# A four-layer decoder trunk on one core: the residual held with features on partitions

## The chip, the core and the metric

The kernel runs on one core of a Trainium2 chip. The core has five engines that run side by side and meet at semaphores: TensorE (PE, matrix products, with its weight loads shown apart as PEld), VectorE (DVE), ScalarE (ACT), GpSimd (POOL) and SyncE (SP), which here only issues DMAs. Each engine works through its own queue in order. TensorE writes to PSUM, which has eight banks of 512 float32 columns on 128 partitions. The metric is device time in microseconds (us) of one execution.

## The reference, cut to what matters

Input and output are 256 tokens of 1024 features, in float32. Layer 0 and layer 3 mix tokens by retention, layer 1 by block attention (with 256 tokens it is plain causal attention), layer 2 by differential attention.

```python
for i in range(DEPTH):                       # 4 layers
    h = _rmsnorm(x, norm1[i])                # over the 1024 features of a token
    m = mixer_i(h)                           # retention, attention, differential attention, retention
    x = x + m                                # m = (...) @ w_out
    x = x + _squared_relu_mlp(_rmsnorm(x, norm2[i]), w_up[i], w_down[i])

def _squared_relu_mlp(h, w_up, w_down):      # 1024 -> 4096 -> 1024
    u = jax.nn.relu(h @ w_up)
    return (u * u) @ w_down
```

## The kernel before

**Precision.** Every weight matrix is read in float32 and split on the chip into a high part (`whi`, ACT, line 170) and a rest (`wlo`, DVE, line 180). Each product takes three passes (`passes`, lines 323 to 326): high by high, high by rest, rest by high. The other operand is split in the same way: `xhi`, `xlo` for the normed input, `uh`, `ul` for the hidden layer, `oh`, `ol` for a mixer's output.

**Weights.** They come in pieces of 128 x 1024 words in a fixed order (`specs`). `advance` lets the split run up to four pieces ahead of the piece that TensorE takes (`take`).

**Products.** Up projection and retention's q and k (`mm_a`) hold a block of weights in the array (128 x 128) and stream the 256 tokens past it: 256 columns for each matmul. The projections to v, gate, q, k, v (`mm_b`) and the down and output projections (`mm_o`) hold a block of activations and stream 512 columns of weights. So `mm_o` leaves its sums (`acc`, four banks) with tokens on partitions, in quarters of 128 tokens x 512 features.

**Residual.** `X` holds 128 partitions x (2 halves of the tokens) x 1024 features. `finish` (lines 436 to 457) runs the last three pieces of a down or output projection quarter by quarter, adds each quarter to `X` on DVE (line 448, or 450 with the factor `r2` of the MLP's norm), and puts off a `norm_quarter` by two ticks. That transposes the quarter on TensorE (line 299, four transposes of 128 x 128 in a stop), and makes `xhi` (ACT, line 302) and `xlo` (DVE, line 305) from the transposed bank. The norm's factor is put in later: for a mixer through `me`, `r2`, `r` (one value for each token, on the token's partition), for an MLP as `r2` in `finish`. `rms` takes the sums of squares on ACT (line 311), each token's along its partition, three ticks after `finish`.

**Order.** The code emits each engine's queue in one pass. `tick()` advances a counter, about once for each piece; `later(n, fn)` puts a step n ticks off, and `at` puts one at a tick counted from the start of an attention layer. Steps due in one tick run in the order of the table `ORDER`. In attention, `softmax` for a pair of heads emits four matmuls (`sc`), four DVE operations that add the bias and take the row's extreme (line 731), and four exponentials on ACT (line 734); the eight pairs start at ticks 12 to 15 and 19, 19, 20, 21. The values `vt` are copied out of PSUM by ACT (line 841) after the projection's last piece, and `av_moba` or `av_diff` on TensorE need them.

Of the kernel before, what the change touches and what calls it, by code (L numbers as in the profile page):

```python
# [31 lines left out]
def trunk(ctx, tc, x_in, rel_bias, norm1, norm2, w_up, w_down, ret_w_in, ret_w_out,  # L32
          moba_w_in, moba_q_norm, moba_k_norm, moba_w_out,
          diff_w_in, diff_q_norm, diff_k_norm, diff_lambda, diff_subln, diff_w_out,
# [5 lines left out]
    const = ctx.enter_context(tc.tile_pool(name="const", bufs=1))  # L40
    op_ = ctx.enter_context(tc.tile_pool(name="op", bufs=1))
    xp = ctx.enter_context(tc.tile_pool(name="xp", bufs=1))
    up_ = ctx.enter_context(tc.tile_pool(name="up", bufs=1))
    wp = ctx.enter_context(tc.tile_pool(name="wp", bufs=1))
# [7 lines left out]
    NRAW, NPC = 3, 6  # L52

# [10 lines left out]
    ORDER = {"av_moba": 0, "av_diff": 0, "probs_t": 1, "softmax": 2, "qk_t": 4, "qk_norm": 5}  # L64
# [21 lines left out]
    def hi_lo(i, a, b, narrow):  # L86
        n = a * b
        hi = wp.tile([P, n], F32R, tag="hi", name="whi", bufs=NPC)
        odd = i % 2
        lo = wp.tile([P, n + (32 if odd else 96)], F32R, tag="lo%d" % (i % NPC), name="wlo", bufs=1)  # L90
        o = 0 if odd == narrow else (32 if odd else 96)
        return (t.rearrange("p (a b) -> p a b", a=a) for t in (hi, lo[:, o:o + n]))

# [66 lines left out]
    def split_piece():  # L160
# [7 lines left out]
        hi, lo = hi_lo(i, a // 2, b, a == 8)  # L168
# [33 lines left out]
    rows = mp.tile([32, P], F32, tag="t2k", name="rows", bufs=4)  # L202
    X = const.tile([P, 2, D], F32, name="X")
    xf = x_in.rearrange("b s d -> (b s) d")
    warm = const.tile([P, 1], F32, name="warm")
    junk = const.tile([P, D], mybir.dt.bfloat16, name="junk")
# [6 lines left out]
    xv = xf.rearrange("(t p) d -> p t d", p=P)  # L213
    ACT.dma_start(rows, norm1.rearrange("l (c p) -> (l c) p", p=P))
    nc.sync.dma_start(X[:, :, 0:S], xv[:, :, 0:S])
    ACT.dma_start(ident, c_ident)
    load_raw(0, 4)
    ACT.activation(warm, warm, AF.Copy)
    for i in range(1, 4):
        nc.sync.dma_start(X[:, :, i * S:(i + 1) * S], xv[:, :, i * S:(i + 1) * S])  # L220
        load_raw(i, 4)
# [5 lines left out]
    nc.sync.dma_start(kd0[:, 2:6, :], rd[:, 2:6, :])  # L227

# [6 lines left out]
    rows2 = mp.tile([64, P], F32, tag="t2k", name="rows2", bufs=4)  # L235

    def small_loads():
        POOL.dma_start(rb, rel_bias)
        POOL.memset(rows2, 0.0)
        POOL.dma_start(rows2[0:32, :], norm2.rearrange("l (c p) -> (l c) p", p=P))  # L240
        for i, w in enumerate((moba_q_norm, moba_k_norm, diff_q_norm, diff_k_norm)):
            for g in range(2):
                POOL.dma_start(rows2[32 + i:33 + i, g * HD:(g + 1) * HD], w)
        POOL.dma_start(rows2[36:37, :], diff_subln)

    W = const.tile([P, 96], F32, name="W")
    wps = aux_bank("wps")
    PE.transpose(wps[:, :32], rows, ident[:32, :32])
    DVE.tensor_copy(W[:, :32], wps[:, :32])
# [3 lines left out]
    def head_weights():  # L253
        wps2 = aux_bank("wps2")
        PE.transpose(wps2[:, :64], rows2, ident[:64, :64])
        DVE.tensor_copy(W[:, 32:96], wps2[:, :64])
# [9 lines left out]
    def small(name, shape):  # L266
        return mp.tile(shape, F32, tag="sm_" + name, name=name, bufs=3)
# [25 lines left out]
    def norm_quarter(l, which, c, t):  # L293
        tt = slice(t * P, (t + 1) * P)
        for pair in range(2):
            ps = aux_bank("xt")
            for i in range(2):
                k = c * 4 + pair * 2 + i
                PE.transpose(ps[:, i * P:(i + 1) * P], X[:, t, k * P:(k + 1) * P], ident)
            for i in range(2):  # L300
                k = c * 4 + pair * 2 + i
                ACT.activation(st["hi"][:, k, tt], ps[:, i * P:(i + 1) * P], AF.Copy, scale=wn(l, which, k))
            for i in range(2):
                k = c * 4 + pair * 2 + i
                DVE.scalar_tensor_tensor(st["lo"][:, k, tt], ps[:, i * P:(i + 1) * P], wn(l, which, k),
                                         st["hi"][:, k, tt].bitcast(F32), op0=OP.mult, op1=OP.subtract)

    def rms(which):
        ss = small("ss", [P, 2])
        for t in range(2):  # L310
            ACT.activation(junk, X[:, t, :], AF.Square, accum_out=ss[:, t:t + 1])
        me = small("me", [P, 2])
        POOL.tensor_scalar(me, ss, 1.0 / D, EPS, op0=OP.mult, op1=OP.add)
# [4 lines left out]
        if which == 0:  # L318
            r = small("r", [P, 2])
            rsqrt(r, me, "r", POOL)  # L320
            st["r"] = r
# [20 lines left out]
    def first_qk(ps):  # L342
# [4 lines left out]
        def turn(pr):  # L347

            bank = aux_bank("xt")
            for i in range(2):  # L350
                for t in range(2):
                    c0 = i * S + t * P
                    k = 2 * pr + i
                    PE.transpose(bank[:, c0:c0 + P], X[:, t, k * P:(k + 1) * P], ident)
            for i in range(2):
                k = 2 * pr + i
# [546 lines left out]
```

## Time and profile before

| | |
|---|---|
| median of 3 runs | 1349.3 us (1347.78 to 1349.87) |
| the profiled execution, time | 1350.42 us |
| its span, first to last instruction | 1348.6 us |
| TensorE busy | 1335.3 us (99%) |
| VectorE busy | 840.4 us (62%) |
| ScalarE busy | 688.2 us (51%) |
| mean granted clock | 0.997 |

The profiled execution took 1.1 us more than the median, and 1.8 us of it lie outside its span. In the trace a matmul's duration is longer than the distance to the next one, because matmuls follow each other in the array before the earlier is through; what a stream of them costs is read from the distance of their starts. A row of a timeline gives start, duration, engine, line, operation, `out<-in` tiles, shapes and count, and in brackets how long the engine had been idle before and what ended that.

### The profile page before, as it was taken

The page shows a single profiled execution, that of the slowest core. Times are in us where ns is not written, and L with a number is a line of the kernel's source. Part 1 is how long each engine was busy: PE and PEld are TensorE (multiplying, and loading weights), DVE is VectorE, ACT ScalarE, POOL GpSimd, SP SyncE. Part 2 cuts the span into 40 slices and gives each one's busy share as a digit, 9 for nine tenths or more (in the row PEclk, how much of TensorE's full clock was granted, in tenths as well). Part 3 has the DMA queues.
Part 4 walks back from the last instruction along what each step waited for, and adds up shares of the span by engine and source line. Part 5 has one row for each costly group of instructions (what it writes and reads, how often), then busy time and mean ns, then how long its engine had stood idle before and what let it go on. Part 6 is the DMA issues. An engine that isn't in the chain of part 4 may idle for free.

```text
span 1348.6 us, 19835 instructions
## 1 busy us (share of the span) xinstructions
PE 1335.3 (99%) x8029; PEld 1170.5 (87%) x8029; DVE 840.4 (62%) x1235; ACT 688.2 (51%) x1058; POOL 109.6 (8%) x314
## 2 busy tenths in 40 slices
PE   9999999999999999999999999999999999999998
PEld 7888889999987679999987789999988888899997
DVE  6666647555568756555578676555667675565554
ACT  5454436444456646444466754444455444554442
POOL 3111100000031000000021110000031011000000
PEclk9999999999999999999999999999999999999999
DMA  8544565555554346555554346555564555465551
GB/s 299 186 163 159 182 193 168 196 198 199 202 202 150 125 125 223 187 188 188 187 173 140 125 147 226 189 188 188 179 205 144 183 172 188 149 225 199 191 189 63
DMA packets 141389, 242.28 MB, mean 180 GB/s; under 512 B 4336, under 2 KB 89024, under 8 KB 141296
## 3 DMA queue, kind: packets, MB, share of 16 engines
q1 hardware_dynamic: 139248, 237.78, 52.7%
q0 software_dynamic: 1072, 2.35, 0.6%
q8 instruction: 63, 1.03, 0.3%
q10 hardware_dynamic: 976, 0.87, 0.2%
q14 instruction: 30, 0.25, 0.1%
HBM read 239.91 MB, written 1.07 MB: 179 GB/s over the span
## 4 chain that ended last, share of the span: by engine, by line
PE 93%; DVE 3%; ACT 2%; DMA 1%; issue 1%; DVEq 0%; ACTq 0%
PE acc L324 12%; PE acc L325 12%; PE acc L326 12%; PE up L325 9%; PE up L326 9%; PE up L324 9%; PE vg L324 4%; PE vg L326 4%; PE vg L325 4%; PE qkv L324 2%; PE qkv L326 2%; PE qkv L325 2%; PE qk L324 2%; PE qk L325 2%; PE qk L326 2%; ACT e L734 1%
## 5 line engine op out<-in xcount | busy, mean ns | idle before, releaser
L180 DVE TENSOR_TENSOR wlo<-raw,whi 128x1024 fp32r<-128x1024 f32 (+1 forms) x448 | 527.3, 1217 | 107.3 <-ACT whi L170 99.5
L170 ACT ACTIVATE whi<-raw 128x1024 fp32r<-128x1024 f32 (+1 forms) x448 | 449.9, 1048 | 88.8 <-PE acc L326 66.7
L324 PE MATMUL up<-xhi,whi 128*128 128x256 f32 x1024 | 283.9, 277 | 0.0
L325 PE MATMUL up<-xlo,whi 128*128 128x256 f32 x1024 | 283.7, 277 | 0.0
L326 PE MATMUL up<-xhi,wlo 128*128 128x256 f32 x1024 | 283.4, 277 | 0.0
L324 PE MATMUL acc<-whi,uu 128*128 128x512 f32 x512 | 200.0, 391 | 0.0
L325 PE MATMUL acc<-wlo,uu 128*128 128x512 f32 x512 | 199.6, 390 | 0.0
L326 PE MATMUL acc<-whi,uu 128*128 128x512 f32 x512 | 199.6, 390 | 0.0
L325 PEld LDWEIGHTS up<-xlo,whi 128*128 128x128 f32 x1024 | 192.3, 188 | 2.2
L324 PEld LDWEIGHTS up<-xhi,whi 128*128 128x128 f32 x1024 | 192.3, 188 | 2.2
L326 PEld LDWEIGHTS up<-xhi,wlo 128*128 128x128 f32 x1024 | 192.5, 188 | 0.0
L466 DVE SCALAR_TENSOR_TENSOR u<-up,u 128x512 f32<-128x512 f32 x64 | 44.2, 691 | 203.3 <-ACT u L465 203.1
L465 ACT ACTIVATE u<-up 128x512 f32<-128x512 f32 x64 | 38.0, 595 | 240.6 <-PE up L326 240.6
L326 PEld LDWEIGHTS acc<-whi,uu 128*128 128x128 f32 x512 | 96.1, 188 | 20.3
L324 PEld LDWEIGHTS acc<-whi,uu 128*128 128x128 f32 x512 | 96.2, 188 | 17.7
L325 PEld LDWEIGHTS acc<-wlo,uu 128*128 128x128 f32 x512 | 96.1, 188 | 17.7
L324 PE MATMUL vg<-whi,xhi 128*128 128x512 f32 x256 | 100.6, 393 | 0.0
L325 PE MATMUL vg<-wlo,xhi 128*128 128x512 f32 x256 | 99.9, 390 | 0.2 <-DVE wlo L180 0.2
L326 PE MATMUL vg<-whi,xlo 128*128 128x512 f32 x256 | 99.8, 390 | 0.0
L324 PE MATMUL qkv<-whi,xhi 128*128 128x512 f32 x192 | 79.0, 411 | 0.0
L324 PE MATMUL acc<-whi,oh 128*128 128x512 f32 x192 | 76.5, 398 | 0.0
L326 PE MATMUL qkv<-whi,xlo 128*128 128x512 f32 x192 | 75.6, 394 | 0.0
(228 smaller groups left out, 1808.0 us busy)
## 6 DMA issues: line engine op xcount, KB each, us to landing
raw<-in_w_up_dram SPq DMA_DIRECT2D x64, 1024.0 KB, 5.6
raw<-in_w_down_dram SPq DMA_DIRECT2D x64, 1024.0 KB, 6.1
raw<-in_ret_w_in_dram SPq DMA_DIRECT2D x45, 1024.0 KB, 5.2
raw<-in_ret_w_out_dram SPq DMA_DIRECT2D x16, 1024.0 KB, 4.9
raw<-in_moba_w_in_dram SPq DMA_DIRECT2D x12, 1024.0 KB, 5.2
raw<-in_diff_w_in_dram SPq DMA_DIRECT2D x12, 1024.0 KB, 5.2
raw<-in_moba_w_out_dram SPq DMA_DIRECT2D x4, 1024.0 KB, 4.9
raw<-in_diff_w_out_dram SPq DMA_DIRECT2D x4, 1024.0 KB, 4.8
```

Source lines behind the costliest of these rows:

```text
L170: ACT.activation(hi[:, part], half[:, part], AF.Copy)
L180: DVE.tensor_tensor(lo[:, part], half[:, part], hi[:, part].bitcast(F32), op=OP.subtract)
L324: PE.matmul(ps, lhsT=ah, rhs=bh, start=first, stop=False, skip_group_check=True)
L325: PE.matmul(ps, lhsT=ah, rhs=bl, start=False, stop=False, skip_group_check=True)
L326: PE.matmul(ps, lhsT=al, rhs=bh, start=False, stop=last, skip_group_check=True)
L465: ACT.activation(u, ps, AF.Relu)
L466: DVE.scalar_tensor_tensor(u, ps, 0.0, u, op0=OP.max, op1=OP.mult)
L734: ACT.activation(e[:, hh, :], e[:, hh, :], AF.Exp, bias=nm[:, qt, hh:hh + 1], scale=-1.0, accum_out=sm[:, qt, hh:hh + 1])
```

## The change

- `x` is handed over transposed (`x_t`), and the output is transposed back on the host. `X` is 128 partitions x 8 blocks of features x 256 tokens, all through. The norms' weights come as one array (`cols`) that is already laid out by partition; the small loads and transposes for them are gone.
- `mm_o` now holds a 128 x 128 block of weights and streams 256 tokens, as `mm_a` does: 24 matmuls of 256 columns for a piece instead of 12 of 512. `acc` has features on partitions, and `finish` goes by quarters of two blocks of features.
- The transposes of the norm are gone. `norm_part` makes `xhi` and `xlo` straight from `X`, in `finish` itself, right behind the quarter's addition; `squares` squares the quarter on ACT.
- The sum over features now runs across partitions. `rms` adds the four squared quarters on DVE, and `rms_sum`, one tick later, has TensorE sum over partitions with a matrix of ones: for an MLP one matmul of 256 columns, whose result on all partitions becomes `r2b`; for a mixer two matmuls of one column.
- An MLP's factor `r2b` varies along the free axis, so `finish` takes two DVE operations for a quarter (multiply, add) where one was.
- In attention the bias step (`logits`) and the exponentials (`softmax`) are apart. The first four pairs of heads keep their ticks; of the last four the exponentials move from ticks 19, 19, 20, 21 to 20, 20, 21, 21.
- Pools are laid out anew, some with gaps, and small tiles changed place.

TensorE where retention ends and the MLP begins (`acc` are its banks, `oh`, `ol` retention's output); before, inside `finish`:

```order
L325 MATMUL acc<-wlo,oh 128x512
L326 MATMUL acc<-whi,ol 128x512
L299 MATMUL xt<-ident,X 128x128 x4
L324 MATMUL acc<-whi,oh 128x512
L325 MATMUL acc<-wlo,oh 128x512
```

And after the change, in the middle of the first block of the up projection, 24 matmuls behind `finish`:

```order
L333 MATMUL up<-xhi,whi 128x256
L334 MATMUL up<-xlo,whi 128x256
L335 MATMUL up<-xhi,wlo 128x256
L315 MATMUL ms<-sq,ones 128x256
L333 MATMUL up<-xhi,whi 128x256
```

The four stops for transposes are gone from the stream, and one matmul on the sums of squares stands in it, ahead of the other half of the up projection's first block.

DVE where layer 1's MLP ends and layer 2 begins (`lam`, `ld`, `nl` belong to the differential factor); before, from the last quarter's addition on:

```order
L450 SCALAR_TENSOR_TENSOR X<-acc,r_4851,X 128x512
L305 SCALAR_TENSOR_TENSOR xlo<-xt,W,xhi 128x128 x4
L642 SCALAR_TENSOR_TENSOR junk,ld<-lam 128x64 x2
L646 TENSOR_TENSOR nl<-ld 128x1
L647 TENSOR_SCALAR nl<-nl 128x1
L305 SCALAR_TENSOR_TENSOR xlo<-xt,W,xhi 128x128 x4
L180 TENSOR_TENSOR wlo<-raw,whi 128x1024 x4
```

After the change:

```order
L446 TENSOR_TENSOR sc<-acc,r2b 128x512
L447 TENSOR_TENSOR X<-X,sc 128x512
L296 SCALAR_TENSOR_TENSOR xlo<-X,W,xhi 128x256 x2
L643 SCALAR_TENSOR_TENSOR junk,ld<-lam 128x64 x2
L647 TENSOR_TENSOR nl<-ld 128x1
L648 TENSOR_SCALAR nl<-nl 128x1
L308 TENSOR_TENSOR sq<-sq 128x512 x3
L309 TENSOR_TENSOR sq<-sq 128x256
L323 TENSOR_SCALAR me<-ms 128x2
```

The four additions of squares stand behind everything else of the last quarter, and `ms`, on TensorE, needs the last of them.

ACT around the first copy of the values in layer 1 (`kT` are the last keys, `e` exponentials, `oh` the first pair's output); before:

```order
L707 ACTIVATE kT<-qkT,W 128x4x128 x2
L734 ACTIVATE e,sm<-e,nm 128x128 x2
L734 ACTIVATE e,sm<-e,nm 128x256 x2
L734 ACTIVATE e,sm<-e,nm 128x128 x2
L734 ACTIVATE e,sm<-e,nm 128x256 x2
L170 ACTIVATE whi<-raw 128x1024
L841 ACTIVATE vt<-qkv,r 128x512 x2
L783 ACTIVATE oh<-oT 128x256
```

After:

```order
L708 ACTIVATE kT<-qkT,W 128x4x128 x2
L176 ACTIVATE whi<-raw 128x1024
L847 ACTIVATE vt<-qkv,r 128x512 x2
L789 ACTIVATE oh<-oT 128x256
L741 ACTIVATE e,sm<-e,nm 128x128 x2
L741 ACTIVATE e,sm<-e,nm 128x256 x2
```

Eight exponentials have moved from ahead of the copy to behind it.

The core of the diff:

```diff
-    def norm_quarter(l, which, c, t):
-        ... (transposes on PE, xhi on ACT, xlo on DVE from the bank)
+    def norm_part(l, which, q):
+        for k in (2 * q, 2 * q + 1):
+            ACT.activation(st["hi"][:, k, :], X[:, k, :], AF.Copy, scale=wn(l, which, k))
+        for k in (2 * q, 2 * q + 1):
+            DVE.scalar_tensor_tensor(st["lo"][:, k, :], X[:, k, :], wn(l, which, k),
+                                     st["hi"][:, k, :].bitcast(F32), op0=OP.mult, op1=OP.subtract)
+
+    def squares(q):
+        sq = mp.tile([P, 512], F32, tag="pe", name="sq", bufs=9)
+        ACT.activation(sq, X[:, 2 * q:2 * q + 2, :].rearrange("p k s -> p (k s)"), AF.Square)
+        st["sq", q] = sq
 
     def rms(which):
-        ss = small("ss", [P, 2])
+        ss = st["sq", 0]
+        for q in range(1, 4):
+            DVE.tensor_tensor(ss, ss, st["sq", q], op=OP.add)
+        DVE.tensor_tensor(ss[:, :S], ss[:, :S], ss[:, S:], op=OP.add)
+        later(1, rms_sum, which, ss)
+
+    def rms_sum(which, ss):
+        ps = aux_bank("ms")
+        if which == 1:
+            PE.matmul(ps[:, :S], lhsT=ones, rhs=ss[:, :S], start=True, stop=True)
+            DVE.tensor_scalar(r2b, ps[:, :S], 1.0 / D, EPS, op0=OP.mult, op1=OP.add)
+            DVE.reciprocal(r2b, r2b)
+            return
         for t in range(2):
-            ACT.activation(junk, X[:, t, :], AF.Square, accum_out=ss[:, t:t + 1])
+            PE.matmul(ps[:, t:t + 1], lhsT=ss[:, t * P:(t + 1) * P], rhs=ones[:, 0:1], start=True, stop=True,
+                      skip_group_check=True)
...
-    def mm_o(q, piece, src, first, last):
-        c, t = q
+    def mm_o(c, piece, src, first, last):
+
         hi, lo = piece
         uh, ul = src
-        tt = slice(t * P, (t + 1) * P)
-        cc = slice(c * 512, (c + 1) * 512)
-        passes(st["acc"][q], uh[:, tt], ul[:, tt], hi[:, 0, cc], lo[:, 0, cc], first, last)
+        cc = slice(c * P, (c + 1) * P)
+        half = slice(c % 2 * S, (c % 2 + 1) * S)
+        passes(st["acc"][c // 2][:, half], hi[:, 0, cc], lo[:, 0, cc], uh, ul, first and c % 2 == 0, last and c % 2 == 1)
...
-        for q in QUARTERS:
+        for q in range(4):
             for i, (pc, src) in enumerate(zip(pcs, srcs)):
-                mm_o(q, pc, src, False, i == len(srcs) - 1)
...
+                for c in (2 * q, 2 * q + 1):
+                    mm_o(c, pc, src, False, i == len(srcs) - 1)
+            xs = X[:, 2 * q:2 * q + 2, :]
+            ps = st["acc"][q].rearrange("p (k s) -> p k s", k=2)
+            if mlp_out:
+                sc = mp.tile([P, 2, S], F32, tag="t2k", name="sc", bufs=4)
+                DVE.tensor_tensor(sc, ps, r2b.unsqueeze(1).to_broadcast([P, 2, S]), op=OP.mult)
+                DVE.tensor_tensor(xs, xs, sc, op=OP.add)
+            else:
                 DVE.tensor_tensor(xs, ps, xs, op=OP.add)
...
-                later(2, norm_quarter, nxt_norm[0], nxt_norm[1], c, t)
+                norm_part(nxt_norm[0], nxt_norm[1], q)
+                squares(q)
             tick()
         if nxt_norm is not None:
-            later(3, rms, nxt_norm[1])
+            later(1, rms, nxt_norm[1])
...
-        SM0, AV0 = ((12, 13, 14, 15), (19, 19, 20, 21)), (20, 24)
+        LG, EX, AV0 = ((12, 13, 14, 15), (19, 19, 20, 21)), ((12, 13, 14, 15), (20, 20, 21, 21)), (20, 24)
```

## Rows read from the trace of the kernel before

**Rows 1.** The page: busy time by engine, and the chain's shares.

```profile
PE 1335.3 (99%) x8029; PEld 1170.5 (87%) x8029; DVE 840.4 (62%) x1235; ACT 688.2 (51%) x1058; POOL 109.6 (8%) x314
...
PE 93%; DVE 3%; ACT 2%; DMA 1%; issue 1%; DVEq 0%; ACTq 0%
```

**Rows 2.** Timeline, TensorE in an MLP: first matmuls of three neighbouring groups.

```profile
260.50 0.39 PE L324 MATMUL acc<-whi,uu 128*128 128x512 f32 x1
...
265.96 0.28 PE L324 MATMUL up<-xhi,whi 128*128 128x256 f32 x1
...
271.43 0.39 PE L324 MATMUL acc<-whi,uu 128*128 128x512 f32 x1
```

**Rows 3.** Timeline, TensorE in retention: second matmul of 48, and what follows.

```profile
53.75 0.28 PE L325 MATMUL qk<-xlo,whi 128*128 128x256 f32 x1
...
59.35 0.39 PE L324 MATMUL vg<-whi,xhi 128*128 128x512 f32 x1
```

**Rows 4.** Timeline, TensorE from retention to the MLP of layer 0.

```profile
199.85 0.60 PE L299 MATMUL xt<-ident,X 128*128 128x128 f32 x4
200.21 0.47 PE L324 MATMUL acc<-whi,oh 128*128 128x512 f32 x1
200.52 0.39 PE L325 MATMUL acc<-wlo,oh 128*128 128x512 f32 x1
...
206.37 0.68 PE L299 MATMUL xt<-ident,X 128*128 128x128 f32 x4
206.80 0.37 PE L324 MATMUL up<-xhi,whi 128*128 128x256 f32 x1
```

**Rows 5.** Waits of TensorE (us in total, times, longest).

```profile
PE oT L778 <- ACT vt L841: 2.6, 1, 2.6
PE od L797 <- ACT vt L841: 2.5, 1, 2.5
```

**Rows 6.** Timeline, ACT ahead of the first copy of values in layer 1.

```profile
449.20 0.40 ACT L734 ACTIVATE e<-e,nm 128x128 f32<-128x128 f32 x1 [2.19 <-DVE nm L731]
...
453.67 1.24 ACT L841 ACTIVATE vt<-qkv,r 128x512 f32<-128x512 f32 x2
```

**Rows 7.** Windows behind both waits: PE, PEld, DVE, ACT, POOL busy, granted clock (PEclk), DMA, GB/s.

```profile
456.10:459.50 3.40, 3.40 (x10) 2.60 (x9) 3.30 (x19) 2.81 (x9) 0.00 (x0) 0.50 0.85 304
...
749.70:753.00 3.30, 3.30 (x17) 3.30 (x17) 0.44 (x1) 0.92 (x5) 0.00 (x0) 0.50 0.55 139
```

**Rows 8.** Timeline, DVE: the second addition behind TensorE's quarter, layer 0.

```profile
200.05 0.69 DVE L448 TENSOR_TENSOR X<-acc,X 128x512 f32<-128x512 f32 x1 [1.35 <-PE acc L326]
```

**Rows 9.** Groups by line and shape, DVE (count, busy us, mean ns of one).

```profile
L471 DVE TENSOR_TENSOR uu<-u,uu 128x512 fp32r<-128x512 f32 x64 | 44.4, 693 | 44.7 <-ACT uu L470 44.7
...
L448 DVE TENSOR_TENSOR X<-acc,X 128x512 f32<-128x512 f32 x16 | 11.1, 692 | 17.6 <-PE acc L326 17.6
...
L746 DVE SCALAR_TENSOR_TENSOR e<-e,dc 128x256 f32<-128x256 f32 x8 | 3.8, 480 | 0.0
...
L784 DVE TENSOR_TENSOR ol<-oT,oh 128x256 fp32r<-128x256 f32 x8 | 3.4, 424 | 10.0 <-ACT oh L783 10.0
```

**Rows 10.** The same view, ACT.

```profile
L357 ACT ACTIVATE xhi<-xt,W 128x256 fp32r<-128x256 f32 x8 | 3.4, 472 | 4.6 <-PE xt L354 4.6
```

**Rows 11.** Timeline, TensorE: full float32 products, four records of 256 columns, four of 128.

```profile
26.84 1.55 PE L523 MATMUL s<-qk 128*128 128x256 f32 x8 [0.20 <-DVE qk L514]
28.14 0.48 PE L324 MATMUL vg<-whi,xhi 128*128 128x512 f32 x1
```

**Rows 12.** Timeline, DVE: the differential factor at the start of layer 2.

```profile
681.58 0.22 DVE L642 SCALAR_TENSOR_TENSOR junk<-lam 128x64 bf16<-128x64 f32 x1
...
682.54 0.15 DVE L647 TENSOR_SCALAR nl<-nl 128x1 f32<-128x1 f32 x1
```

**Rows 13.** Timeline: the first product of the program (TensorE), the last addition (DVE).

```profile
7.75 0.39 PE L376 MATMUL qk<-xhi,whi 128*128 128x256 f32 x1 [0.96 <-ACT whi L365]
...
1344.46 0.75 DVE L450 SCALAR_TENSOR_TENSOR X<-acc,r,X 128x512 f32<-128x512 f32 x1 [1.29 <-PE acc L326]
```

More of the change, by code (lines that the diff above doesn't have):

```diff
@@ L212, in trunk @@
     DVE.memset(warm, 0.0)
[L213 to L216, printed above, removed]
+    DVE.memset(ones, 1.0)
+    ACT.dma_start(W, cols)
+    nc.sync.dma_start(X[:, 0:2, :], xv[:, 0:2, :])
     load_raw(0, 4)
@@ L317, in rms @@
         st["r2"] = r2
[L318 to L321, printed above, removed]
+        r = small("r", [P, 2])
+        rsqrt(r, me, "r", POOL)
+        st["r"] = r
     def passes(ps, ah, al, bh, bl, first, last):
@@ L347, in turn @@
         def turn(pr):
[L349 to L356, printed above, removed]
-                ACT.activation(st["hi"][:, k, :], bank[:, i * S:(i + 1) * S], AF.Copy, scale=wn(0, 0, k))
-            for i in range(2):
-                k = 2 * pr + i
-                DVE.scalar_tensor_tensor(st["lo"][:, k, :], bank[:, i * S:(i + 1) * S], wn(0, 0, k),
-                                         st["hi"][:, k, :].bitcast(F32), op0=OP.mult, op1=OP.subtract)
+            norm_part(0, 0, pr)
             hi, lo = pieces[pr // 2]
@@ L431, in out_piece, with finish @@
         pc = take()
-        for q in QUARTERS:
-            mm_o(q, pc, src, first, False)
+        for c in range(KC):
+            mm_o(c, pc, src, first, False)
         tick()
-    def finish(srcs, r2, nxt_norm):
+    def finish(srcs, mlp_out, nxt_norm):
         advance(4, 4)
@@ L494, in mlp @@
             else:
-                finish([U[14][1]] + U[15], st["r2"], (l + 1, 0) if l + 1 < DEPTH else None)
+                finish([U[14][1]] + U[15], True, (l + 1, 0) if l + 1 < DEPTH else None)
     def retention(l):
-        OT = {}
+        OL = [op_.tile([P, 4, S], F32R, tag="ol%d" % h, name="ol") for h in range(RH)]
+        if l == 0:
+            fill = op_.tile([P, 64], F32, name="fill")
+            nc.vector.memset(fill[:, 0:1], 0.0)
+        OT = list(zip([op_.tile([P, 4, S], F32R, tag="ot%d" % h, name="oh") for h in range(RH)], OL))
         if l == 0:
@@ L733, in softmax @@
                                              -1.0, 3e38, OP.add, OP.min, accum_out=nm[:, qt, hh:hh + 1])
[L734 to L735 removed]
+            at(EX[b][i], softmax, p, E, nm)
+        def softmax(p, E, nm):
+            sm = mp.tile([P, 2, 2], F32, tag="smx", name="sm", bufs=12)
+            for qt in range(2):
+                for hh in range(2):
+                    e = E[qt][:, hh, :]
+                    ACT.activation(e, e, AF.Exp, bias=nm[:, qt, hh:hh + 1], scale=-1.0, accum_out=sm[:, qt, hh:hh + 1])
             SM[p] = sm
```

139 lines of the change are left out of this document (60 added, 79 removed).

## The prediction

> **What bounds the kernel now.** I read the page's busy times and chain first: TensorE is busy for 99% of the span, and the chain that ended last runs on it for 93% [rows 1]. So a microsecond that TensorE stands, or works on something new, is one of the result, and work on DVE and ACT counts only where TensorE waits for it. Next the timeline of TensorE in an MLP, for the rate: 24 matmuls of 512 columns take 260.50 to 265.96, 5.46 us, and 48 of 256 take 265.96 to 271.43, 5.47 us [rows 2]. That is 0.2275 and 0.114 us apart: one price for a column, though the second form loads twice as many weights. Then the places where the stream breaks: the norms' transposes [rows 4] and TensorE's list of waits, which has two of weight, both on ACT's copy of the values [rows 5].
>
> **Projections with stationary weights.** 12 matmuls of 512 columns become 24 of 256 for a piece; by [rows 2] 5.46 us stay 5.47 us. An MLP then streams 256 columns all through. One part of each group is dearer than its steady run: 48 x 0.1133 would be 5.44 us, so the pair of groups has 0.05 us of change-over, 64 pairs, 3.2 us in all. I take 2 us of gain, from 0 to 3.2. Against it stands [rows 3]: retention's q and k, the same shape, take 5.60 us for 47 matmuls, 0.119 apart at full clock. So operands of one shape can run 5% apart, and which pace the new pairs take no row shows. The nearest row is the up projection's, whose form and order of passes they copy.
>
> The Trainium skill (SBUF — State Buffer, "SBUF: two separate sides") says that TensorE waits for no other user of the SBUF, and that its two reads are independent; by that the slow pace could not come from the operands' places, and the new products would keep 0.114. Rows 3 show the slow pace all the same, so I keep it as a rival.
>
> **The transposes go.** One stop takes 199.85 to 200.21, and the matmul behind it 0.31 instead of 0.23; the last takes 0.43 and 0.10 more [rows 4]. Four such are 0.44 + 0.44 + 0.44 + 0.53, with the uneven matmuls behind them 2.0 us for a norm. Seven norms: -14.0 us (-13 to -15). In the first norm TensorE's first product waits for transposes and ACT until 7.75 [rows 13]; without the transposes ACT starts on X as it lands, and three more stops fall away. I take -1.7 us, from 0 (the weights' DMAs set the pace behind it, and this norm's `ms`, 72 matmuls in, may wait a little) to -2.5.
>
> **Attention.** TensorE waits 2.6 and 2.5 us for the values [rows 5]. ACT does eight exponentials from 449.20 on and a split ahead of the copy at 453.67 [rows 6]; they move behind it, and the copy then starts when the projection ends. Some 0.4 us (half of the copy's 1.24, less what the first bank has ahead) stay: -2.2 and -2.1. Behind each wait TensorE's granted clock is 0.50, the 1.2 GHz level, for 3.4 us, after having stood for most of 3 us [rows 7]; half of 3.3 us, some 1.6, comes back each time: -3.2 us. Sum -7.5 us (-3 to -9). The same exponentials now stand ahead of two more splits, which run four pieces ahead; that covers them. Without the cover a late split costs up to 1 us.
>
> **The new wait.** It decides the forecast. `ms` stands on TensorE behind the first 24 matmuls of a phase (12 of 512 columns in an attention layer), 2.72 us after `finish` ends, and everything else of TensorE is queued behind it. It needs the last addition of squares on DVE. Let T0 be the end of the last quarter's products.
>
> *From mixer to MLP* (four times): DVE's addition starts 0.2 us after TensorE has gone on (200.05 against 199.85) [rows 4, 8] and takes 0.69; ACT makes two blocks of xhi, 0.47 each [rows 10]; DVE ends the second xlo 0.48 later. That is 2.11 for a quarter, while TensorE takes 18 x 0.1133 = 2.04, so DVE is 0.2 late at the last one. Then three additions of 0.69 and one of 0.42 [rows 9], 2.49 together. Ready: 0.2 + 0.2 + 2.11 + 2.49 = T0 + 5.0. TensorE stands 2.3 us. `ms` itself is a full float32 product: four records of 256 and four of 128 columns take 1.30 us [rows 11], so a record of 256 is 0.217 and the two of this matmul 0.43, with 0.1 for the restart. 2.8 us each, +11.3 us.
>
> *From MLP to mixer* (three times): two operations of 0.69 where one was. A quarter takes DVE 2.80, and it falls 0.76 behind in each of three: it begins the last at T0 + 2.5, ends it at T0 + 5.3, and the sums at T0 + 7.8. In layer 1 an addition on the bias stands between (about 0.5) and one product of 0.7 ahead on TensorE: it stands 4.9. In layer 2 the differential factor stands between, 681.58 to 682.69, 1.1 us [rows 12]: 6.2. In layer 3: 7.8 - 2.8 = 5.0. `ms` is four records of one column, at most 0.1 each, say 0.4 with the restart: 16.1 + 1.2 = +17.3 us.
>
> The lower bound comes from the work that cannot be put elsewhere: with DVE never late and the first two additions done early, last addition 0.69 (1.38), xhi twice, a square of some 0.6 and two additions of 1.1 put `ms` at T0 + 3.5 (4.2), and both terms shrink to 4 x 1.3 + 3 x 1.9 = 11 us. The upper one adds 0.5 us to each for handing over between engines, 32 us.
>
> *The clock.* Two waits of 2.5 and 2.6 us were each followed by half clock [rows 7]; the one of 1.0 us at the start was not [rows 13]. The three long ones will be, 1.6 us each; of the four of 2.3 I take two: 8 us (0 to 11.2).
>
> What is behind the wait is not late: the next splits need 2 x 1.2 us of DVE, and TensorE still has 24 matmuls ready. `r2b` takes two operations of 256 columns, of which the trace shows no reciprocal that wide; up to 0.8 us is covered there, more would cost up to 1 us four times.
>
> **The end.** Two operations for one behind the last product: 2 x 0.69 against 0.75 [rows 9, 13], +0.6 us. SP's queue keeps its order, and POOL loses small loads that nothing waited for.
>
> **Sum.** -2 - 14.0 - 1.7 - 7.5 + 11.3 + 17.3 + 8 + 0.6 = +12.0 us. On the profiled execution's 1350.4 that is 1362.4; it took 1.1 us more than the median of the runs, 1349.3, so I give 1361.
>
> **Rivals.** *The sums are in time* (faster): the one mechanism is that DVE and ACT overlap more than their durations laid end to end, so that the chain is at its lower bound. Then the new wait costs 11 us instead of 28.6, no wait comes near those of rows 5, and the clock stays: 12.0 - 17.6 - 8 = -13.6, some 1336. It decides from the point where the two terms of `ms` and the clock together fall under 24.6 us. For it: TensorE's distances show that durations overlap there. Against it: DVE's queue is in order, the additions stand last in it, and for a row that waits on another engine there is nothing to overlap with. 0.17. *A draw*: the stalls as in the sum less a quarter, and clock falls behind the long ones only: 28.6 x 0.75 + 4.8 = 26.3, against 24.6: 1351. 0.15. *The slow pace*: the projections run at 0.119: 3072 + 1152 matmuls x 0.0055 = 23 us more, 1384. For it: rows 3; against it: the copied form. 0.07. *The exponentials only move the wait*: ACT, now behind, holds up the transposed probabilities instead, 7 us of gain are lost, 1368. 0.08.
>
> By another rule the transposes are worth more. In the trace they start 0.11 us apart and 112 of them with all they break cost 14 us [rows 4]. The Trainium skill (TensorE: Matmul & The Clock Gate, "Part 4: PE-mode transpose") gives some 275 ns for one inside a kernel; 112 would be an estimated 31 us, the sum -5 us and the time 1344. The trace shows that as a duration and not as a distance, so: 0.03.
>
> **How the numbers follow.** The forecast has 0.50. A change under 0.2% (2.7 us) can't be told from none here. Faster takes the first rival and the rule's, 0.20; within 0.2% most of the draw, 0.12; slower the rest, 0.68. The range goes from 1335, which takes in the first rival, to 1374, above the moved exponentials and the forecast with its upper bounds for wait and clock. It leaves out the slow pace (0.07) and what may add up beyond the bounds, about as much again at either end.
>
> **What would show it.** In the timeline after: `ms` on TensorE with idle time ahead that DVE's `sq` ends, 2.3 us at four places and 5 to 6 at three; DVE's four additions as the last before it; half clock behind the long ones; `od` and `oT` with a short wait for the values; 48 matmuls of a piece pair in 5.44 us; no `xt`. I am wrong if `ms` starts without idle time ahead of it, or if the down projection's matmuls lie other than 0.113 to 0.114 apart.

## The result, and the profile after

The changed kernel takes 1373.3 us (median of four runs, 1371.7 to 1373.9), the kernel before 1348.7 beside it: a ratio of 1.018, with a 95% interval of 1.0167 to 1.0194. The change costs 24.7 us. The forecast was slower, by 12 us, to 1361; the time lies at the upper end of the range. All comparisons of stages below are made between the profiled executions, 1350.4 before and 1373.7 after, 23.3 us apart.

The page's busy times and its chain, to be read against [rows 1]:

```profile
PE 1331.1 (97%) x10035; PEld 1249.1 (91%) x10035; DVE 868.2 (63%) x1237; ACT 684.9 (50%) x1002; POOL 110.7 (8%) x295
...
PE 88%; DVE 6%; ACT 3%; DMA 1%; issue 1%; SPq 0%; DVEq 0%; ACTq 0%
```

TensorE has less work (1331 us of it where 1335 were) in a span that is 23 us longer. Its share fell from 99 to 97%, and DVE has twice its former share of the chain (6% for 3%): TensorE now stands for DVE. The list of TensorE's waits (us in total, times, longest) names the places; the lines of the values, [rows 5], have shrunk from 2.6 and 2.5 to the last two.

```profile
PE ms L320 <- DVE sq L309: 20.1, 4, 6.5
PE ms L315 <- DVE sq L309: 8.9, 4, 2.3
...
PE oT L831 <- ACT pT L770: 1.0, 1, 1.0
...
PE od L803 <- ACT pT L770: 0.5, 1, 0.5
...
PE oT L784 <- ACT vt L847: 0.2, 1, 0.2
PE od L803 <- ACT vt L847: 0.2, 1, 0.2
```

For 29.0 us TensorE stands ahead of `ms`. The timeline shows them one by one, with the idle time ahead in brackets: the start, the first MLP, layers 1 to 3 (two of the four MLPs are left out, 2.28 and 2.27).

```profile
19.18 0.61 PE L320 MATMUL ms<-ones,sq 128*128 128x1 f32 x4 [2.99 <-DVE sq L309]
...
211.29 0.70 PE L315 MATMUL ms<-sq,ones 128*128 128x256 f32 x2 [2.18 <-DVE sq L309]
...
392.88 1.01 PE L320 MATMUL ms<-ones,sq 128*128 128x1 f32 x4 [5.05 <-DVE sq L309]
...
694.97 1.01 PE L320 MATMUL ms<-ones,sq 128*128 128x1 f32 x4 [6.52 <-DVE sq L309]
...
994.60 0.98 PE L320 MATMUL ms<-ones,sq 128*128 128x1 f32 x4 [5.55 <-DVE sq L309]
...
1193.03 0.70 PE L315 MATMUL ms<-sq,ones 128*128 128x256 f32 x2 [2.18 <-DVE sq L309]
```

What DVE does meanwhile, at the entry of layer 1 (its last quarter, then the bias and the sums; the layer's own first product starts at 384.8):

```profile
386.92 0.69 DVE L446 TENSOR_TENSOR sc<-acc,r2b 128x512 f32<-128x512 f32 x1
387.64 0.69 DVE L447 TENSOR_TENSOR X<-X,sc 128x512 f32<-128x512 f32 x1
388.90 0.88 DVE L296 SCALAR_TENSOR_TENSOR xlo<-X,W,xhi 128x256 fp32r<-128x256 f32 x2 [0.58 <-ACT xhi L294]
389.70 0.54 DVE L630 TENSOR_TENSOR gs<-gps,msk 16x384 f32<-16x384 f32 x1
390.17 2.19 DVE L308 TENSOR_TENSOR sq<-sq 128x512 f32<-128x512 f32 x3
392.40 0.42 DVE L309 TENSOR_TENSOR sq<-sq 128x256 f32<-128x256 f32 x1
```

It begins the MLP's last quarter 2.1 us after TensorE has gone on to layer 1, and a quarter takes it 2.79 us, 0.58 of them idle for ACT's xhi. The windows behind the waits (columns as in [rows 7]) show the clock: at or near 0.50 behind the three long ones (layers 1 and 2 are shown) and behind one of the four short ones, 1.00 behind the other three, of which the last line is one.

```profile
394.40:397.80 3.40, 3.40 (x10) 2.63 (x9) 3.40 (x4) 0.13 (x1) 3.19 (x5) 0.50 0.96 261
696.00:699.40 3.40, 3.40 (x9) 2.69 (x10) 3.34 (x5) 0.77 (x1) 2.87 (x4) 0.57 0.02 5
...
1193.90:1197.30 3.40, 3.40 (x18) 3.40 (x17) 3.37 (x4) 0.29 (x1) 0.00 (x0) 0.50 0.00 0
211.20:214.60 3.40, 3.31 (x27) 3.26 (x28) 2.58 (x4) 1.25 (x2) 0.00 (x0) 1.00 0.00 0
```

By the starts of the first product of each stage, in both timelines, the difference to the kernel before is this (us; the last four columns belong to experiments below):

| stage | after | late | behind | POOL | best |
|---|---|---|---|---|---|
| start and layer 0's mixer | +2.2 | +1.9 | +5.2 | +1.8 | -0.2 |
| layer 1's attention | +4.2 | +2.9 | +1.2 | +3.7 | -3.8 |
| layer 2's attention | +7.0 | +6.0 | +4.0 | +1.9 | -0.2 |
| layer 3's retention | +7.8 | +3.6 | +7.4 | +1.2 | 0.0 |
| four output projections | -5.2 | -5.2 | -5.2 | -5.2 | -5.2 |
| four MLPs | +7.2 | -3.8 | -3.8 | -3.7 | -3.6 |
| sum | +23.3 | +5.3 | +8.8 | -0.2 | -12.9 |

A norm's `ms` is charged to the stage that begins with it.

### The profile page after: what moved, and what is told of

Its sections match the earlier page's. It is cut to its first block, busy times and chain, and to the rows that moved or that the text cites. A ratio compares the mean times of both kernels' runs of the same rounds, so it can differ in the third digit from the quotient of the medians.

```text
span 1371.9 us, 23860 instructions
## 1 busy us (share of the span) xinstructions
PE 1331.1 (97%) x10035; PEld 1249.1 (91%) x10035; DVE 868.2 (63%) x1237; ACT 684.9 (50%) x1002; POOL 110.7 (8%) x295
## 3 DMA queue, kind: packets, MB, share of 16 engines
q8 instruction: 78, 1.28, 0.4%
## 4 chain that ended last, share of the span: by engine, by line
PE 88%; DVE 6%; ACT 3%; DMA 1%; issue 1%; SPq 0%; DVEq 0%; ACTq 0%
PE acc L333 10%; PE acc L334 10%; PE acc L335 10%; PE up L335 8%; PE up L333 8%; PE up L334 8%; PE vg L333 4%; PE vg L335 4%; PE vg L334 4%; PE qkv L333 3%; PE qkv L334 3%; PE qkv L335 3%; PE qk L333 2%; PE qk L334 2%; PE qk L335 2%; DVE xlo L296 2%
## 5 line engine op out<-in xcount | busy, mean ns | idle before, releaser
L334 PE MATMUL acc<-uu,whi 128*128 128x256 f32 x1024 | 282.7, 276 | 0.0
L333 PE MATMUL acc<-uu,whi 128*128 128x256 f32 x1024 | 282.6, 276 | 0.0
L335 PE MATMUL acc<-uu,wlo 128*128 128x256 f32 x1024 | 282.6, 276 | 0.0
L333 PEld LDWEIGHTS acc<-uu,whi 128*128 128x128 f32 x1024 | 192.2, 188 | 0.0
L335 PEld LDWEIGHTS acc<-uu,wlo 128*128 128x128 f32 x1024 | 192.2, 188 | 0.0
L334 PEld LDWEIGHTS acc<-uu,whi 128*128 128x128 f32 x1024 | 192.2, 188 | 0.0
L333 PE MATMUL acc<-oh,whi 128*128 128x256 f32 x384 | 106.9, 278 | 0.0
L334 PE MATMUL acc<-ol,whi 128*128 128x256 f32 x384 | 106.1, 276 | 0.0
L335 PE MATMUL acc<-oh,wlo 128*128 128x256 f32 x384 | 106.1, 276 | 0.0
```

The lines of the kernel that those rows point to most:

```text
L333: PE.matmul(ps, lhsT=ah, rhs=bh, start=first, stop=False, skip_group_check=True)
L334: PE.matmul(ps, lhsT=ah, rhs=bl, start=False, stop=False, skip_group_check=True)
L335: PE.matmul(ps, lhsT=al, rhs=bh, start=False, stop=last, skip_group_check=True)
```

## Experiments

**ms later.** The changed kernel, with `ms` two or three ticks further behind on TensorE ("late" in the table).

```diff
-        later(1, rms_sum, which, ss)
+        later(4 if which == 0 else 3, rms_sum, which, ss)
```

> Here ms is issued later: on TensorE it stands behind 60 products of 512 columns or 120 of 256 in a mixer and behind 72 of 256 in an MLP, some 8 to 13 us after the last product of the layer before, where 2.7 us stood. Theory A, the waits ahead of ms: the sums of DVE are ready 5.0 to 9.4 us after that last product in the trace of the changed kernel, so all eight waits (29.0 us in its list of waits) fall away and with them the stretches at granted clock 0.50 behind five of them, 9.4 us by the distances between matmuls (1.69 + 2.34 + 1.53 + 1.85 + 1.97). 1373.3 - 29.0 - 9.4 = 1335, faster than the kernel before. Theory B, DVE is what is late: it does the sums at the same time as now, and the splits behind them then come late instead; TensorE waits for wlo where it waited for sq. A split takes DVE 1.22 us and a piece 2.72 us of TensorE, four pieces ahead, so at most a part of a wait comes back; with half of them back the time is 1354. The list of waits tells the two apart: by A it holds no sq and no more wlo than the 1.2 us of now.

1353.7 us, 1.0036 of the kernel before (1.0024 to 1.0047). No `sq` is left in the list of waits; these came in its stead:

```profile
PE qkv L334 <- DVE wlo L186: 5.3, 2, 2.7
PE vg L334 <- DVE wlo L186: 3.0, 1, 3.0
PE qkv L333 <- ACT whi L176: 2.1, 2, 1.9
PE qk L335 <- DVE wlo L186: 1.8, 2, 1.5
```

The MLPs give all of it back, 11 us, and there theory A holds. In the mixers and at the start theory B does: of 20 us of wait and 7 of clock only 7.0 come back. DVE's rows at the entry of layer 1, whose first product starts at 381.9, show why:

```profile
387.30 2.19 DVE L308 TENSOR_TENSOR sq<-sq 128x512 f32<-128x512 f32 x3
389.53 0.42 DVE L309 TENSOR_TENSOR sq<-sq 128x256 f32<-128x256 f32 x1
389.87 6.89 DVE L186 TENSOR_TENSOR wlo<-raw,whi 128x1024 fp32r<-128x1024 f32 x6
```

`finish` has taken three pieces at once, so two are ready when a mixer begins, 5.4 us of TensorE; the third is split at 391.1, 9.2 us into the layer. The sums in DVE's queue hold up TensorE with `ms` or without it.

**The sums behind the splits.** `ms` of the MLPs late as above, and the sums of the mixers and of the first norm three, and two, ticks later ("behind"), with `ms` one tick behind them.

```diff
-            later(1, rms, nxt_norm[1])
+            later(1 if nxt_norm[1] == 1 else 4, rms, nxt_norm[1])
...
-        later(1, rms_sum, which, ss)
+        later(3 if which == 1 else 1, rms_sum, which, ss)
...
-    later(3, rms, 0)
+    later(5, rms, 0)
```

> The run with a late ms showed DVE's queue: it issues the sums ahead of six splits, and TensorE then waits for wlo. Here the three mixers' sums (and those of the first norm) are issued some three ticks later too, behind five of these splits; ms stands behind them. Theory A, the order in DVE's queue makes the wait: in layer 1 the last xlo ends 5.0 us after the last product, an addition on the bias and a split end 1.7 us later, and the third piece needs it at 5.6, so some 1.2 us of wait stay, 2.2 in layer 2 (the differential factor comes first), 1.5 in layer 3, about 1 at the start, none long enough for half clock in the runs so far (but layer 2's). From 1353.7 that takes away 5 + 5 + 1.5 + 4: 1338. Theory B, DVE as a whole is short of time here: the wait only goes to a later piece or to the sums, and the time stays within 4 us of 1353.7.

1360.2 us, 1.0088 (1.0073 to 1.0103): slower than the run before, and both theories missed. The waits for wlo are shorter than A put them (0.8 us each in layers 1 and 2, 0.4 at the start), but `ms` waits again, 10.6 us in three places: 5.6 at the start, 1.5 in layer 1 and 3.4 in layer 3. In layer 2 the wait is for whi, 1.9 us. TensorE at the start, and DVE at the entry of layer 1:

```profile
27.37 1.02 PE L320 MATMUL ms<-ones,sq 128*128 128x1 f32 x4 [5.64 <-DVE sq L309]
```

```profile
391.27 5.76 DVE L186 TENSOR_TENSOR wlo<-raw,whi 128x1024 fp32r<-128x1024 f32 x5 [0.53 <-ACT whi L176]
396.96 2.13 DVE L308 TENSOR_TENSOR sq<-sq 128x512 f32<-128x512 f32 x3
```

Five splits, 5.76 us, now stand ahead of the sums, more work than the 2.6 us of sums that stood ahead of the splits. That the order in the queue decides who waits, as A has it, is not shown by this run alone; the sums in the middle, below, bear it out.

**xlo a quarter behind.** The changed kernel; DVE makes xlo of a quarter behind the next quarter's addition on X.

```diff
                 norm_part(nxt_norm[0], nxt_norm[1], q)
                 squares(q)
+                for b in ((q - 1,) if q in (1, 2) else (2, 3) if q == 3 else ()):
+                    norm_lo(nxt_norm[0], nxt_norm[1], b)
```

> The changed kernel with one thing else: in the last four quarters of a layer DVE makes xlo of a quarter after the addition on X of the next, not at once; sums and ms stand where the change put them. In the trace DVE idles 0.58 us in each quarter for ACT's xhi, and a quarter takes it 2.79 us where TensorE takes 2.04. Theory A, as the prediction's sum has it (DVE falls behind by 0.76 a quarter because of this round trip): without it a quarter takes 2.2 us, the last xlo of a layer ends at 3.7 us after the last product instead of 5.0 to 5.3, and the three waits of ms in the mixers get 1.5 to 1.7 us shorter; the MLPs' (0.69 + 0.9 + 0.85 behind the last product either way) don't. 1373.3 - 5 = 1368. Theory B, the lag comes from the amount of DVE's work: no wait changes by more than 0.3 us, 1373.

1366.9 us, 1.0136 (1.0121 to 1.0152), 6.5 less than the changed kernel, where A gave 5. The same quarter of DVE, with layer 1's first product at 384.8 again:

```profile
384.38 0.68 DVE L449 TENSOR_TENSOR sc<-acc,r2b 128x512 f32<-128x512 f32 x1
385.09 0.69 DVE L450 TENSOR_TENSOR X<-X,sc 128x512 f32<-128x512 f32 x1
385.70 1.67 DVE L298 SCALAR_TENSOR_TENSOR xlo<-X,W,xhi 128x256 fp32r<-128x256 f32 x4
...
389.98 0.42 DVE L311 TENSOR_TENSOR sq<-sq 128x256 f32<-128x256 f32 x1
```

DVE starts the last quarter 0.5 us ahead of that product instead of 2.1 behind it, and the sums are ready at 390.4 instead of 392.8. The waits of the start and the mixers fall from 20.1 to 12.7 us, the MLPs' stay (9.1). A quarter takes DVE 2.12 us instead of 2.79, TensorE 2.04. So nearly all of the prediction's lag of 0.76 us a quarter was the round trip by way of ACT, not the amount of DVE's work.

**TensorE kept busy during the wait.** Extra products ahead of each `ms`, which change nothing in its operands.

```diff
+        for _ in range(fills[which].pop(0)):
+            PE.matmul(ps[:, :S], lhsT=filler[:, :P], rhs=filler, start=True, stop=True, skip_group_check=True)
```

> The changed kernel with extra bfloat16 products of 256 columns on zeros ahead of each ms (26, 46, 60 and 52 ahead of the four of the mixers' norms, 20 ahead of each of the MLPs'), so that TensorE works through the time in which it stood. ms comes no sooner, and the output is the same. If the slow stretches behind the waits are the clock's, brought on by standing, they go: 1373.3 - 9.4 = 1364, with the granted clock at 0.97 to 1.00 behind every ms. If they come from something else behind ms (operands that arrive late, contention), the time stays at 1373, or goes up by what the extra products overrun the waits, 1 to 2 us.

1365.7 us, 1.0118 (1.0102 to 1.0134): 7.7 us less than the changed kernel, with 264 extra products, 0.110 us apart. The same window behind layer 1's `ms` as above stands at full clock, as nearly all of the span does (0.999 in the mean):

```profile
394.40:397.80 3.40, 3.40 (x17) 2.81 (x16) 3.40 (x4) 1.06 (x1) 3.15 (x4) 1.00 1.00 293
```

So half clock follows from TensorE's standing, and its price is a term of its own: 7.7 us by the medians, 9.4 by the two profiled spans. The rest of the wait's price is the wait.

**Exponentials back.** The changed kernel with `EX` equal to `LG`.

```diff
-        ... EX ... (20, 20, 21, 21))
+        ... EX ... (19, 19, 20, 21))
```

> The changed kernel with the exponentials of the last four head pairs back at the ticks of their logits, as before; all else as changed. If the prediction's step on attention is right, the two waits for the values return (2.6 and 2.5 us in the trace before, 0.2 and 0.2 in that of the changed kernel) and with each some 1.5 us at half clock behind it; the waits of layer 2 for the transposed probabilities (1.0 and 0.5 us) go. 1373.3 + 2.4 + 2.3 + 3.0 - 1.5 = 1379.5. If the exponentials only move the wait, as the rival has it, the time stays within 2 us of 1373.3.

1379.6 us, 1.0226 (1.0206 to 1.0246), as expected in sum. The waits return whole, and those for pT are gone:

```profile
PE oT L784 <- ACT vt L847: 2.6, 1, 2.6
PE od L803 <- ACT vt L847: 2.6, 1, 2.6
```

Not in its parts: in the profiled execution only layer 2's wait is followed by half clock (0.61 in the window behind it, 1.00 in layer 1's), and two short waits of `ms` have it where one had. By stages the exponentials are worth 2.1 us in each attention layer of that execution.

**The exponentials alone.** The kernel before with `softmax` cut in two as in the change, at its ticks, and nothing else (a diff like the change's own).

> The kernel before with the third part of the change alone: exponentials apart from logits, those of the last four head pairs at the later ticks. If its gain doesn't hang on the other parts: the waits for the values (2.6 and 2.5 us) and the half clock behind them go in both attention layers, 3.75 us in layer 1; in layer 2 a wait for the transposed probabilities takes 2.3 of 3.7 back, as in the changed kernel: 1349.4 - 5.2 = 1344. If they depend on what else the change moved, it stays within 2 us of 1349.4.

1346.0 us, 0.998 of the kernel before (0.9971 to 0.9989), 2.9 us less by the medians and 3.7 by the stages of the profiled executions, where 5.2 were expected. By stages layer 1 gains 3.8 us and layer 2 1.3, and both stand as expected; 1.3 us are lost at the start, before any of the edit has run, where this execution waits 1.2 us for the rotated queries and keys ahead of the scores, and that of before 0.2 [rows 11]; what makes this wait longer is not shown. This part of the change is a gain without the others.

**The operand's place.** The changed kernel, with uh and ul elsewhere in their tile.

```diff
-            uh, ul = (... for o in (576, 0))
+            uh, ul = (... for o in (592, 80))
```

> The changed kernel with the two halves of the squared ReLU (uh, ul), the operand that moves through TensorE in the down projection, at other places of their tile: 592 and 80 words in where 576 and 0 stood. Both then have the places (modulo 512 bytes) that xhi and xlo have in retention's q and k, whose products of 256 columns run 0.119 apart; as changed they have those of the up projection's, 0.113 apart. Nothing else moves. If the operands' places set the pace, the 3072 products of the down projection go from 0.1134 to 0.119 apart: + 17 us, 1390. If TensorE's reads don't depend on places, as the prediction quotes the Trainium skill (SBUF - State Buffer), the time stays 1373.

1393.8 us, 1.0332 (1.0312 to 1.0352): 20 us more by a shift of some words. Twelve starts of the down projection, in the changed kernel first:

```profile
235.73 0.28 PE L333 MATMUL acc<-uu,whi 128*128 128x256 f32 x1
...
236.97 0.28 PE L335 MATMUL acc<-uu,wlo 128*128 128x256 f32 x1
```

```profile
235.81 0.28 PE L333 MATMUL acc<-uu,whi 128*128 128x256 f32 x1
...
237.11 0.28 PE L335 MATMUL acc<-uu,wlo 128*128 128x256 f32 x1
```

Eleven distances take 1.24 us there and 1.30 here, 0.113 and 0.118. From start to start all 3072 products take 365 us where they took 348, 17 us as expected. The up projection's products between them, whose operands did not move, take 5.6 us more: in this execution three of the MLPs' four short waits are followed by half clock (granted clock 0.50 or 0.51) instead of one, which makes 3.0 of the 5.6; the mixers take 2 us less. TensorE's list of waits has none for `uu`, so the pace is not that of an operand that comes late. The rival of the slow pace was real, and the change avoids it by its offsets. The Trainium skill (SBUF — State Buffer, "SBUF: two separate sides") has TensorE wait for nobody and its two reads independent of each other. That their places don't matter was inferred from that, and the page speaks of no places; here the measurement decides, and the other place costs 5%.

**The sums on POOL.** `ms` late, xlo a quarter behind, the mixers' sums on POOL ("POOL" in the table).

```diff
+        eng = POOL if which == 0 else DVE
...
-            DVE.tensor_tensor(ss, ss, st["sq", q], op=OP.add)
+            eng.tensor_tensor(ss, ss, st["sq", q], op=OP.add)
```

> The changed kernel with the sums of squares for the mixers' norms (the first one's too) on POOL instead of DVE, ms as late as in the first run, and xlo a quarter behind; the MLPs' sums stay on DVE, the exponentials as changed. DVE's splits then have nothing ahead of them but xlo. If DVE's queue was what held TensorE up, the waits for wlo and sq go (each mixer's under 1 us, none at half clock). Worked out by stages against the kernel before: start -1.7, four output projections -1.3 each, MLPs -1.5 (three) and +0.7, layer 1 -4, layer 2 -1.5, layer 3 about +0.5: -16, 1333. If POOL's additions of 512 columns take it much longer than DVE's 0.69 us or slow DVE down beside them, ms waits for POOL: more than 2 us at each of four places, over 1345.

1348.8 us, 0.9997 (0.9987 to 1.0006), no difference to the kernel before. The forecast of over 1345 for slow additions came true in the time, but not in its places: `ms` waits for POOL at one place and not at four. Layer 1's rows, DVE's six splits, and POOL's loads of the bias and three additions:

```profile
385.31 9.87 DVE L186 TENSOR_TENSOR wlo<-raw,whi 128x1024 fp32r<-128x1024 f32 x6 [0.41 <-ACT whi L176]
```

```profile
387.51 3.05 POOL L640 DMA_DIRECT2D bt<-gd  x4 [1.83 <-DMA gd<-gs]
390.58 5.73 POOL L311 TENSOR_TENSOR sq<-sq 128x512 f32<-128x512 f32 x3
```

Six splits take 9.87 us where they took 6.89, an addition 1.9 where DVE takes 0.7, and `ms` waits 4.1 us for POOL here. Slow additions are only a part of that: ACT ended the last square at 384.3, and POOL, which had the bias ahead in its queue from 385.2 on, began to add at 390.6. At the other three places POOL has no such work ahead and `ms` does not wait for it. So once more it is what stands ahead in the queue. Layer 2's rows show what an addition on POOL does to DVE:

```profile
684.41 1.28 POOL L311 TENSOR_TENSOR sq<-sq 128x512 f32<-128x512 f32 x1 [2.16 <-ACT sq L303]
```

```profile
684.56 1.21 DVE L649 SCALAR_TENSOR_TENSOR junk<-lam 128x64 bf16<-128x64 f32 x1
```

The same operation on 64 columns takes DVE 0.21 us just before. The Trainium skill (SBUF — State Buffer, "SBUF: two separate sides") says that DVE with two inputs in SBUF and GpSimd shut each other out; the rows agree: DVE's small operation ends 0.1 us after POOL's addition, and in layer 1 3 us are lost on DVE for 5.7 on POOL.

**The sums in the middle.** xlo a quarter behind as there, but the mixers' sums on DVE behind four splits, `ms` two or three ticks after them; the first norm's stay on POOL.

```diff
-            later(1, rms, nxt_norm[1])
+            later(1 if nxt_norm[1] == 1 else 3, rms, nxt_norm[1])
...
-        later(1, rms_sum, which, ss)
+        later(4 if "me" not in st else 3 if which == 1 or nxt[2] > 300 else 2, rms_sum, which, ss)
```

> As the run before in this list, but the mixers' sums on DVE, behind four of the splits (the earlier run had them behind five and ms one tick after them, and ms waited again), ms two to three ticks after them; only the first norm's sums are on POOL. If each wait comes from what stands ahead in DVE's queue and nothing else, there is now a place for the sums at which nobody waits: layer 1 and 2 under 0.6 us of wait, layer 3 under 1.5, and 1334. If it is DVE's amount of work at a layer's end, some 2.5 us of wait stay in each of the three mixers, half of them with half clock behind, and 1342.

1341.9 us, 0.9947 (0.9932 to 0.9962), faster than both kernels. The time is that of the second theory, 1342, but by chance: the mixers' waits went as the first has it, and of `ms` one wait of 0.4 us is left. What neither theory had is at the start (2.4 us for wlo beside POOL's additions, with half clock behind) and in the queries:

```profile
PE qkT L711 <- DVE qn L701: 2.4, 2, 1.4
PE vg L337 <- DVE wlo L186: 2.4, 1, 2.4
...
PE ms L323 <- DVE sq L312: 0.4, 1, 0.4
```

A combination of the sums behind, xlo behind and one pair of exponentials early came to 1353.2 us (1.0033, 1.0021 to 1.0046): it has the wrong place for the sums, 11.0 us of wait for `sq`, and the early pair brought back 0.9 us for the values in each attention layer.

> All together: ms late, the mixers' sums behind the splits, xlo one quarter behind, and the exponentials of one of the last four head pairs (instead of none) at the tick of its logits, so that layer 2's probabilities come sooner. If the waits found so far are all that the change costs, the mixers' waits fall to under 0.5 us each and those for the transposed probabilities (1.1 + 0.5 us) go: 1338 - 3.5 - 1.5 = 1333, some 16 us faster than the kernel before. If DVE's work as a whole is the limit at the layer's end, it gives no more than the run with the sums behind alone.

**The start, and r.** The first norm's squares among the first splits, and r three ticks later on POOL ("best").

```diff
-        rsqrt(r, me, "r", POOL)
         st["r"] = r
+        later(3, rsqrt, r, me, "r", POOL)
...
-                for _ in range(2):
+                for q in (0, 2):
+                    squares(q)
+                    squares(q + 1)
                     split_piece()
                     split_lo()
```

> The version with the sums in the middle (1341.9) with two waits more taken on. Its list of waits has 2.4 us for wlo at the start, with half clock behind it (1.6 us by the distances), where ACT makes the first norm's four squares (2.2 us) ahead of a split: they are issued here among the first splits, in ACT's two gaps of 0.9 and 1.1 us for a DMA. And it has 2.4 us for the normalized queries (qn), where POOL takes 3.6 us for r = 1/sqrt(me) ahead of the queries' factor: r is issued here three ticks later. If both readings are right: 1341.9 - 2.0 - 1.6 - 2.0 = 1336. If the start is short of DVE's time and not of ACT's order, the first stays and it is 1340.

1338.2 us, 0.9919 (0.9905 to 0.9933), and the mean granted clock is 1.00. The waits for qn are gone, and so is the half clock at the start; there 1.6 and 0.7 us of waits for wlo remain, more than expected.

**The mixers' operands moved too.** As the run before, `xhi` and `xlo` of the mixers at the MLPs' places.

```diff
-        oh, ol = (64, 48) if mlp_in else (80, 0)
+        oh, ol = (64, 48)
```

> As the run before in this list, with xhi and xlo of the mixers at the places that they have in the MLPs (64 and 48 words in instead of 80 and 0). If the place of the operand that moves sets the pace of 256-column products, as the run with uh and ul elsewhere showed, retention's 768 products of q and k go from 0.119 to 0.1133 apart: - 4.4 us against the run before. The products of vg and qkv, in which xhi and xlo are the weights and whi and wlo move, keep 0.227 if the place of the operand that moves decides alone; if it is the two places together, they may lose: 1344 products by some 0.006 would be + 8 us.

1337.2 us, 0.9912 (0.9898 to 0.9926), 1.0 us less, under what can be told. The stretch of [rows 3], 47 products of q and k, takes 5.36 us instead of 5.60:

```profile
54.42 0.28 PE L337 MATMUL qk<-xlo,whi 128*128 128x256 f32 x1
...
59.78 0.39 PE L336 MATMUL vg<-whi,xhi 128*128 128x512 f32 x1
```

But the products of vg and qkv, 512 columns, go from 0.227 to 0.229 apart in the mean. In these products only the weights' places changed. So the place of the operand that moves doesn't decide alone; how the two combine is not shown.

## Why the prediction came out as it did

The direction, and the mechanism that decides it, stood as foretold: `ms` behind DVE's sums. The size didn't: 12.0 us by the sum, 23.3 between the profiled executions. That the time lies in the range is in part luck, for its upper end was laid for the moved exponentials and for longer waits and more half clock at seven norms, and the largest miss came at the eighth. Step by step:

- **From mixer to MLP.** 2.3 us of standing foretold, 2.18 to 2.28 measured; with `ms` and the restart 0.6 each instead of 0.5, +11.3 as foretold.
- **From MLP to mixer.** 4.9, 6.2 and 5.0 foretold, 5.05, 6.52 and 5.55 measured. `ms` itself takes 0.9 us rather than 0.4, since its records run at half clock (granted clock 0.50 from 392.85 on in layer 1). +19.8 for +17.3. Laying the durations of a queue end to end was right here, and the rival that DVE and ACT overlap more was not.
- **The start.** This is the term that failed. The prediction took 1.7 us of gain and let `ms` of the first norm "wait a little". The gain is there (the first product starts at 5.95 instead of 7.75), but `ms` waits 2.99 us, and 1.7 us of half clock lie behind it: with `ms` itself, 5 us that the sum didn't have. ACT makes the four squares only behind the first splits (from 15.2 to 17.4), and DVE's sums of 2.7 us end at 19.1. It was worked out for seven norms, and there are eight.
- **Attention.** -7.5 foretold, -5.2 measured. Layer 1 has it all (3.75 us). In layer 2 the rival of the moved wait held in part. ACT, behind with eight exponentials of two head pairs and two splits, copies the transposed probabilities late, and TensorE waits 1.0 and 0.5 us for it:

```profile
774.07 2.00 ACT L176 ACTIVATE whi<-raw 128x1024 fp32r<-128x1024 f32 x2
775.97 0.84 ACT L770 ACTIVATE pT<-pT 128x384 f32<-128x384 f32 x2
```

- **The clock.** +8 foretold. By the distances between matmuls, against those at full clock, it is 7.7 behind the three long waits and one short one, and 1.7 at the start; the run with TensorE kept busy gives 7.7 to 9.4 in all. Only the start was missing, but that the rest fits is partly chance: the three long waits cost 5.7 us instead of 4.8, and one short one came instead of two, at 2.0. Which of the short waits are followed by half clock isn't settled: both before, one of four after, three of six with the exponentials back, three of the MLPs' four with the operand elsewhere.
- **Projections and transposes.** -2 and -14. The distances of the projections' products give -2.3 (down 349.6 to 348.2 us, outputs 133.0 to 132.1). The transposes: in the trace before, the 28 stops cost TensorE 0.44 to 0.54 us each by the distances around them, 13.0 us in all. What the other terms leave of the 23.3 us is -12; the difference is in three new waits of 0.4 us for wlo, some 4 us behind `ms` in three of the MLPs. The 31 us of the other rule are ruled out.
- **The end.** +0.6 foretold; from the last product's start to the end of the span it is 5.4 us for 4.6, +0.8.
- **What is behind the wait.** "Not late", said the prediction, and but for those three waits the trace after agrees. In the mixers it was so only because TensorE stood: with `ms` late the splits are. `r2b` takes 0.42 us and, for the reciprocal, 1.75, not up to 0.8; nobody waits for it.

The 11.3 us between sum and measurement are then 5.0 at the start, 2.3 in layer 2, 2.5 in the mixers' waits and 2 in the transposes and the new waits for wlo, less some tenths.

## What to carry to other kernels

Work that is moved to an engine with 40% of its time free can still cost what it was to save: what counts is what stands in that engine's queue at the moment when the bottleneck comes by. When a product waits for a chain of small steps, first move the product, then look for who stood in the shadow of the wait, and only then move the chain; here the first step alone gave 20 us, and all of them together 35 against the changed kernel. And when something is done once for each of N places, count the first and the last of them by themselves.

## What the runs showed of the hardware

- The place of TensorE's operands in SBUF sets the pace of a float32r product of 256 columns, 0.113 or 0.119 us, and of one of 512, 0.227 or 0.229. Shifts of 16 and 80 words were worth 17 us in the down projection.
- Additions on POOL beside splits on DVE slow both: six splits go from 6.89 to 9.87 us, and an addition of 512 columns on POOL takes 1.28 us at the least, 1.5 in the mean and 2.13 at worst.
- A reciprocal of 256 columns on DVE takes 1.75 us, an operation with two constants on the same columns 0.42:

```profile
212.03 0.42 DVE L316 TENSOR_SCALAR r2b<-ms 128x256 f32<-128x256 f32 x1 [0.79 <-PE ms L315]
212.49 1.75 DVE L317 RECIPROCAL r2b<-r2b 128x256 f32<-128x256 f32 x1
```
